# A hybrid diffusion backbone in one core: where the eight PSUM banks are divided and joined, and where the modulation stands

## The chip, the cores and the metric

The kernel runs on one core of one Trainium2 chip. The number that counts is the device time of one execution in microseconds (us). For the kernel before it is 2413.35 us, the median of three runs that lie between 2412.6 and 2416.89 us. Below, the execution that was profiled took 2414.47 us; its span, from the first to the last recorded instruction, is 2412.7 us, so 1.8 us of it lie outside the span.

## The reference, cut to what matters

One inference step of a backbone of two layers. 640 tokens (128 of a prompt and 512 of a sample) with 1024 features pass three sub-layers in each layer: a SwiGLU half step, a mixer (attention beside a gated linear scan in layer 0, a chunked gMLP in layer 1) and a second SwiGLU half step. Each sub-layer normalises before and after and is modulated by a condition:

```python
def rmsnorm(x, g):
    xf = x.astype(jnp.float32)
    y = xf * lax.rsqrt(jnp.mean(xf * xf, axis=-1, keepdims=True) + EPS)
    return (y * g.astype(jnp.float32)).astype(x.dtype)

def adaln(cond, w, b):
    return (jax.nn.silu(cond) @ w + b).reshape(-1, N_SUB, 3, D_MODEL)

def sub_in(x, mod, i, g_pre):
    return rmsnorm(x, g_pre) * (1 + mod[:, i, 1][:, None]) + mod[:, i, 0][:, None]

def sub_out(x, y, mod, i, g_post, coef):
    return x + coef * mod[:, i, 2][:, None] * rmsnorm(y, g_post)

def macaron_ffn(x, mod, i, g_pre, g_post, wg, wu, wd):
    h = sub_in(x, mod, i, g_pre)
    y = (jax.nn.silu(h @ wg) * (h @ wu)) @ wd
    return sub_out(x, y, mod, i, g_post, FFN_RESIDUAL)
```

`adaln` gives 9 x 1024 numbers per layer for each of two conditions, in 72 rows of 128 a layer (called f below). Each f needs its own 512 KB of weights.

## The kernel before, in words

Features lie on the 128 partitions, in eight tiles (`KD`); the 640 tokens are cut into half 0 (384) and half 1 (256). Every weight is float32. ACT writes its rounded high part (L100) and DVE the rest (L101) into a buffer `whl` of which there are six, and a product takes three matmuls: high by high (`hh`), high by low (`hl`), low by high.

The order of instructions on each engine is fixed when the program is built. Every engine takes its queue in that order and waits at the first instruction that isn't ready. Nothing overtakes.

A feed-forward sub-layer (`ffn`) runs over groups of channels. The first group begins in `head`: four blocks of weights for half 0 in four banks at once (the joint product, `gemm_joint`), further blocks one by one, then the same for half 1. DVE takes each bank out (`normed`, L595, the first step of an eviction) and builds `g`. The first down phase follows, whose sums ACT copies to `y` for half 0 and DVE for half 1 (L816, L818). Later groups are "fast": they take products in a few passes from operands made by `fast_operands`, and use two sorts of banks. The last down phase is called by `tail`, first all of half 0, then half 1. While half 1 runs, `chain(0)` works on half 0: the statistics (`rstd`: a matmul with `ones`, L384, and two ACT operations, L393 and L394), then for each of eight feature tiles a scaling (L423), an addition to the residual (L459) and the next operands `hh` on ACT (L430) and `hl` on DVE (L435). What is left of it, and `chain(1)` for half 1, run in the `head` of the next sub-layer, between the evictions. A mixer ends in `out_proj`, which goes through `tail` too.

The eight banks of PSUM are one ring of `ps` tiles or, divided, four `ps` and four `sd`. `split_psum` closes the one ring, opens the two and issues four matmuls with one row into the `sd` banks; `whole_psum` closes both and opens the ring of eight. A bank can be written once the last reader of what it held is through. The division stands in `ffn` behind the first down phase, the join behind `tail`, ahead of the next head. So a head finds eight banks, the four of the joint product and four more.

The modulation goes beside all this: `mod_queue` gives for each f a transfer (L318, on SP's queue, two buffers `wmod`) and two DVE operations (`mod_op`, L326, output `junk`), one for each condition. `pace` spreads them over a feed-forward's units; `out_proj` puts its own behind the units of half 0. `mod_derive` (L367 to L372) makes the factors from the sums.

## Time and profile before

| | |
|---|---|
| median of three runs | 2413.35 us (2412.6 to 2416.89) |
| the profiled execution | 2414.47 us, span 2412.7 us |
| PE (TensorE) busy | 2331.8 us, 97% of the span |
| DVE (VectorE) busy | 1852.1 us, 77% |
| ACT (ScalarE) busy | 1290.0 us, 53% |
| POOL (GpSimd) busy | 327.5 us, 14% |
| mean granted TensorE clock | 0.988 |

In a view of an engine's timeline a row gives the start, the busy time, the line and operation, the tiles and the count; in brackets stand the idle time ahead of it and what ended that idle time. Several instructions of one kind in a row are put into one. The waits of an engine are grouped by what waited and what ended the wait. A row of windows gives for one stretch the busy time of each engine, with counts, and the granted TensorE clock (1.00 is the upper of its two levels, 0.50 the lower).

### The profile page before, as it was taken

The numbers are of one execution on the slowest core, as the hardware profiler recorded it, in microseconds if no ns is written. First come the engines' busy times: TensorE is split into PE (matmuls) and PEld (weight loads), VectorE is DVE, ScalarE is ACT, GpSimd is POOL, SyncE is SP. The second block draws the span as 40 slices with busy tenths as digits, with TensorE's granted clock in tenths as the row PEclk, the third lists the DMA queues.
The fourth block names the chain that finished last, engine by engine and source line by source line (L and its number), as shares of the span: only waits on it lengthen the run. The fifth ranks groups of instructions, "written<-read, shape, count | busy, mean of one in ns | idle before, by whom it ended". The sixth has DMA issues, their size and how long they took to land.

```text
span 2412.7 us, 40104 instructions
## 1 busy us (share of the span) xinstructions
PE 2331.8 (97%) x15528; PEld 2268.6 (94%) x15528; DVE 1852.1 (77%) x3347; ACT 1290.0 (53%) x2637; POOL 327.5 (14%) x289
## 2 busy tenths in 40 slices
PE   7899999999999999999999999999999999999998
PEld 5799999999899799999999999999988899999998
DVE  8898889586966698887875788889495797765574
ACT  4555454565546556544556555445574356454555
POOL 5100000041502340000003100000130540000002
PEclk9999999999999999999999999999999999999999
DMA  8334544431021343353533333443334343332332
GB/s 300 100 120 136 179 136 153 140 126 59 19 77 45 121 143 117 120 174 110 180 123 132 119 109 126 163 151 121 123 123 148 111 135 111 108 114 68 100 97 105
DMA packets 87569, 297.85 MB, mean 123 GB/s; under 512 B 9681, under 2 KB 15313, under 8 KB 84305
## 3 DMA queue, kind: packets, MB, share of 16 engines
q1 hardware_dynamic: 86082, 292.07, 37.0%
q8 instruction: 121, 1.98, 0.3%
q10 hardware_dynamic: 864, 2.17, 0.2%
q0 software_dynamic: 432, 1.05, 0.2%
q14 instruction: 70, 0.57, 0.1%
HBM read 276.25 MB, written 19.01 MB: 122 GB/s over the span
## 4 chain that ended last, share of the span: by engine, by line
PE 65%; DVE 21%; DMA 6%; ACT 4%; issue 3%; POOL 1%; SPq 0%; DVEq 0%; ACTq 0%; POOLq 0%
PE ps L199 35%; PE sd L199 30%; DVE junk L326 4%; DVE whl L101 3%; DMA wmod<-in_wmod 2%; DVE y L423 2%; DVE hl L435 1%; ACT whl L100 1%; DVE hl L631 1%; DMA wraw<-in_wgu 1%; DMA wraw<-in_wd 1%; DMA b<-xspill 1%; DVE b L625 1%; DVE x L459 1%; DMA wraw<-in_wdl 1%
## 5 line engine op out<-in xcount | busy, mean ns | idle before, releaser
L199 PE MATMUL ps<-hh,whl 128*128 128x320 f32 (+4 forms) x4128 | 955.1, 316 | 18.2 <-ACT y L816 8.7
L101 DVE TENSOR_TENSOR whl<-wraw,whl 128x1024 fp32r<-128x1024 f32 (+3 forms) x552 | 531.4, 967 | 328.9 <-ACT whl L100 319.1
L199 PEld LDWEIGHTS ps<-hh,whl 128*128 128x128 f32 x4128 | 710.5, 191 | 25.5 <-ACT y L816 9.3
L199 PE MATMUL ps<-hl,whl 128*128 128x320 f32 (+4 forms) x2064 | 645.1, 313 | 14.5 <-DVE hl L435 13.1
L100 ACT CAST whl<-wraw 128x1024 fp32r<-128x1024 f32 (+3 forms) x552 | 461.5, 839 | 330.1 <-issue 107.4
L199 PE MATMUL sd<-g,whl 128*128 128x384 f32 (+1 forms) x3264 | 482.5, 308 | 5.9 <-DVE g L676 5.3
L199 PEld LDWEIGHTS sd<-g,whl 128*128 128x128 f32 x3264 | 476.9, 188 | 10.4 <-DVE g L676 7.9
L199 PEld LDWEIGHTS ps<-hl,whl 128*128 128x128 f32 x2064 | 395.7, 192 | 19.9 <-DVE hl L435 15.0
L407 POOL TENSOR_TENSOR acc<-acc,tmc 128x384 f32<-128x384 f32 (+1 forms) x154 | 174.4, 1134 | 1766.3 <-ACT tmc L400 1751.2
L199 PE MATMUL sd<-th,whl 128*128 128x320 f32 x2448 | 383.0, 309 | 4.9 <-ACT sd L679 4.9
L199 PEld LDWEIGHTS sd<-th,whl 128*128 128x128 f32 x2448 | 366.2, 188 | 5.7 <-ACT sd L679 5.7
L326 DVE SCALAR_TENSOR_TENSOR junk<-wmod,cbc 128x1024 bf16<-128x1024 f32 x258 | 323.2, 1253 | 30.3 <-DMA wmod<-in_wmod 19.3
L816 ACT COPY y<-sd 128x384 f32<-128x384 f32 (+1 forms) x192 | 80.6, 425 | 113.0 <-PE sd L199 112.9
L199 PE MATMUL ps<-g,whl 128*128 128x384 f32 (+1 forms) x960 | 140.7, 308 | 0.0
L199 PEld LDWEIGHTS ps<-g,whl 128*128 128x128 f32 x960 | 140.1, 188 | 0.3 <-DVE g L743 0.3
L199 PE MATMUL sd<-hh,whl 128*128 128x320 f32 x544 | 131.0, 311 | 0.8 <-DVE tmp L687 0.8
L423 DVE SCALAR_TENSOR_TENSOR y<-y,dm,rstd 128x128 f32<-128x128 f32 (+1 forms) x128 | 70.2, 580 | 34.7 <-ACT rstd L394 34.7
L430 ACT ACTIVATE hh<-x,dm 128x128 fp32r<-128x128 f32 (+1 forms) x144 | 63.5, 468 | 61.1 <-DVE x L459 42.1
L199 PEld LDWEIGHTS sd<-hh,whl 128*128 128x128 f32 x544 | 93.0, 187 | 1.7 <-DVE tmp L687 1.6
L435 DVE SCALAR_TENSOR_TENSOR hl<-x,dm,hh 128x128 fp32r<-128x128 f32 (+1 forms) x144 | 90.1, 656 | 0.7 <-ACT hh L430 0.4
L199 PE MATMUL ps<-whl,hh 128*128 128x320 f32 (+1 forms) x320 | 87.0, 355 | 1.4 <-ACT whl L100 1.4
L786 ACT COPY sd<-y 128x384 f32<-128x384 f32 (+1 forms) x192 | 81.1, 433 | 13.5 <-DVE tmp L690 10.4
(246 smaller groups left out, 2594.2 us busy)
## 6 DMA issues: line engine op xcount, KB each, us to landing
wraw<-in_wgu SPq DMA_DIRECT2D x170, 512.0 KB, 3.8
wmod<-in_wmod SPq DMA_DIRECT2D x130, 512.0 KB, 4.2
wraw<-in_wd SPq DMA_DIRECT2D x64, 320.0 KB, 3.0
xspill<-x SPq DMA_DIRECT2D x12, 1280.0 KB, 4.4
x<-xspill SPq DMA_DIRECT2D x12, 1280.0 KB, 9.2
wraw<-in_wd SPq DMA_DIRECT2D x32, 384.0 KB, 3.8
wraw<-in_wdl SPq DMA_DIRECT2D x24, 512.0 KB, 4.0
b<-xspill SPq DMA_DIRECT2D x16, 640.0 KB, 4.6
```

Source lines behind the costliest of these rows:

```text
L100: k.nc.scalar.copy(w[:, 0, c], raw)
L101: k.nc.vector.tensor_sub(w[:, 1, c], raw, w[:, 0, c])
L199: self.nc.tensor.matmul(out, lhsT, rhs, start=start, stop=stop, **more)
L326: ins = nc.vector.scalar_tensor_tensor(junk, w, 1.0, self.c_bc[:, cond, :], op0=ALU.mult, op1=ALU.mult, accum_out=out)
L407: self.nc.gpsimd.tensor_add(acc, acc, t)
L423: self.nc.vector.scalar_tensor_tensor(self.y[:, m, a:a + ln], src[:, m, a:a + ln], self.mcol(lay, s, which, m, cond), r[:, a - o:a - o + l ...
L430: self.nc.scalar.activation(self.hh[:, k, 2 + a:2 + a + ln], self.x[:, k, a:a + ln], AF.Copy, scale=self.mcol(lay, s, 1, k, cond))
L435: self.nc.vector.scalar_tensor_tensor(self.hl[:, k, 2 + a:2 + a + ln], self.x[:, k, a:a + ln], self.mcol(lay, s, 1, k, cond), self.hh[:, k ...
L459: nc.vector.tensor_add(xs, xs, self.y[:, m, o:o + n])
L625: nc.vector.scalar_tensor_tensor(v, v, self.mcol(lay, s, 1, k + 4 * j, cond), self.r[:, a:a + n], op0=ALU.mult, op1=ALU.mult)
L786: nc.scalar.copy(seeds[m, half][:, :n], self.y[:, m, o:o + n])
L816: nc.scalar.copy(ys, ps[:, :n])
```

## The change

It has three parts. First, `split_psum` stands ahead of the first down phase and no longer behind it, and all sums of that phase are copied by ACT, half 1 too (32 copies move from DVE). Second, `whole_psum` moves out of `ffn` into `head`, ahead of half 1's joint product, if the banks are divided at that point. So half 0 of the three heads that follow a feed-forward sub-layer (of both mixers and of the first half step of layer 1) has four `ps` banks, and the statistics that fall into it take an `sd` bank (`late=True`). The two heads that follow `out_proj` are as they were. Third, `tail` takes a list of modulation steps and puts them behind the units of half 0, with the shifts' operands after them, and the f are dealt out anew:

| place | f before | f after |
|---|---|---|
| ffn(0,0): body, tail | 40, 0 | 32, 5 |
| out_proj(0) | 8 | 11 |
| ffn(0,1): body, tail | 32, 0 | 28, 4 |
| ffn(1,0): body, tail | 32, 0 | 24, 5 |
| out_proj(1) | 8 | 11 |
| ffn(1,1) | 8 | 8 |

```diff
--- before.py
+++ after.py
@@ -376,11 +376,12 @@
         return self.dm[:, j:j + 1]
 
 
-    def rstd(self, half, table, more=None):
+    def rstd(self, half, table, more=None, late=False):
+
 
         nc = self.nc
         n = HALF[half][1]
-        ps = self.ps()
+        ps = self.sd() if late and self.n_sd else self.ps()
         mm = self.nc.tensor.matmul(ps[:, :n], self.ones, self.accs[half], start=True, stop=more is None)
         if more is not None:
             self.mm(ps[:, :n], self.ones, more, False, True)
@@ -448,7 +449,7 @@
 
         nc = self.nc
         o, n = HALF[half]
-        self.rstd(half, 0)
+        self.rstd(half, 0, late=half == 1)
         yield
 
         def f_t(m):
@@ -473,7 +474,7 @@
         if nxt is None:
             return
         yield from self.pipeline(KD, [(0, f_s)])
-        self.rstd(half, 2 if half and nxt != (0, 1) else 0)
+        self.rstd(half, 2 if half and nxt != (0, 1) else 0, late=True)
         yield
 
     def renorm(self, half, nxt):
@@ -523,20 +524,23 @@
                 return
 
 
-    def tail(self, unit, n_blocks, cur, nxt):
+    def tail(self, unit, n_blocks, cur, nxt, mod=()):
 
 
         ws = self.ws
         wis = [ws.next() for _ in range(n_blocks)]
         self.pin(self.nc.scalar.preload_act_table_set(LNEXP))
         ch = [self.chain(0, cur, nxt), self.chain(1, cur, nxt)]
-        if nxt is not None:
-            self.shifts(*nxt)
         both = max(0, n_blocks - NB)
+        mod = list(mod)
         for m in range(KD):
             unit(m, 0, wis)
             if m < both:
                 unit(m, 1, wis)
+            for _ in range(-(-len(mod) // (KD - m))):
+                mod.pop(0)()
+        if nxt is not None:
+            self.shifts(*nxt)
         done = 0
         for m in range(both, KD):
             unit(m, 1, wis)
@@ -578,6 +582,8 @@
                 self.step(ch[1], 99)
             self.step(again[0], 1)
 
+        if self.n_sd:
+            self.whole_psum()
         pss = self.gemm_joint(wis[:joint], self.hacts(1), late)
         self.step(ch[1], 99)
         self.step(again[0], 99)
@@ -694,7 +700,7 @@
         result(tr, sr, r)
 
 
-    def ffn(self, lay, f, ch, mod, nxt, start=None):
+    def ffn(self, lay, f, ch, mod, nxt, start=None, late=()):
         nc, ws = self.nc, self.ws
         s = 0 if f == 0 else 2
         mod = list(mod)[::-1]
@@ -812,13 +818,12 @@
                 end = nxt is None and half == 1
                 if last and not end:
                     self.sq_acc(half, ps[:, :n], m == 0)
-                if gi or half == 0:
-                    nc.scalar.copy(ys, ps[:, :n])
-                else:
-                    nc.vector.tensor_copy(ys, ps[:, :n])
+                nc.scalar.copy(ys, ps[:, :n])
                 if last and end:
                     self.last_part(m, lay, s)
 
+            if gi == 0:
+                self.split_psum()
             if not last:
                 for m in range(KD):
                     wi = ws.next()
@@ -830,14 +835,10 @@
                         self.fast_operands(lay, s, m)
                     else:
                         pace(1)
-                if gi == 0:
-                    self.split_psum()
             else:
                 while mod:
                     mod.pop()()
-                ch = self.tail(down, 6, (lay, s), nxt)
-                self.whole_psum()
-                return ch
+                return self.tail(down, 6, (lay, s), nxt, late)
 
     def open_ffn(self):
         self.g_f, self.fp = self.pool("ffn", side="left")
@@ -1342,11 +1343,9 @@
             ys = self.y[:, m, o:o + n]
             self.sq_acc(half, ps[:, :n], m == 0)
             nc.scalar.copy(ys, ps[:, :n])
-            if half == 0:
-                for _ in range(-(-len(mod) // (KD - m))):
-                    mod.pop(0)()
-
-        return self.tail(unit, KD, (lay, 1), (lay, 2))
+
+        mod.pop(0)()
+        return self.tail(unit, KD, (lay, 1), (lay, 2), mod)
 
 
     def mixer1(self, ch):
@@ -1628,20 +1627,20 @@
             self.mod_load(0)
             self.mod_load(1)
 
-        q = queue(0, (16, 40), (48, 64)) + derive(0, 0, (2,)) + derive(0, 1, (0, 1)) + derive(0, 2, (0, 1))
-        ch = self.ffn(0, 0, None, q, (0, 1), start)
+        q = queue(0, (16, 53))
+        ch = self.ffn(0, 0, None, q[:-10] + derive(0, 0, (2,)) + derive(0, 1, (0, 1, 2)), (0, 1), start, q[-10:])
         self.mixer0(ch)
         self.open_xy()
         self.unspill()
         open_ffn()
-        ch = self.out_proj(0, queue(0, (40, 48)) + derive(0, 1, (2,)))
-        q = queue(0, (64, 72)) + derive(0, 2, (2,)) + queue(1, (0, 24)) + derive(1, 0, (0, 1, 2))
-        ch = self.ffn(0, 1, ch, q, (1, 0))
-        q = queue(1, (24, 40), (48, 64)) + derive(1, 1, (0, 1)) + derive(1, 2, (0, 1))
-        ch = self.ffn(1, 0, ch, q, (1, 1))
+        ch = self.out_proj(0, queue(0, (53, 64)) + derive(0, 2, (0, 1)))
+        q, q1 = queue(0, (64, 72)), queue(1, (0, 24))
+        ch = self.ffn(0, 1, ch, q + derive(0, 2, (2,)) + q1[:-8] + derive(1, 0, (0, 1)), (1, 0), None, q1[-8:] + derive(1, 0, (2,)))
+        q = queue(1, (24, 53))
+        ch = self.ffn(1, 0, ch, q[:-10] + derive(1, 1, (0, 1, 2)), (1, 1), None, q[-10:])
         self.mixer1(ch)
         open_ffn()
-        ch = self.out_proj(1, queue(1, (40, 48)) + derive(1, 1, (2,)))
+        ch = self.out_proj(1, queue(1, (53, 64)) + derive(1, 2, (0, 1)))
         q = queue(1, (64, 72)) + derive(1, 2, (2,))
         ch = self.ffn(1, 1, ch, q, None)
         self.step(ch[0], 99)
```

On DVE in `out_proj(0)` the modulation stands in a row, ahead of the factor for the gate (`dm`), of the first weight block of the next head (`whl_8869`) and of half 0's chain (the `y` and `x` rows). The last rows of it before:

```order
L326 SCALAR_TENSOR_TENSOR junk_8798,modraw<-wmod_8758,cbc_8454 128x1024
L326 SCALAR_TENSOR_TENSOR junk_8834,modraw<-wmod_8758,cbc_8454 128x1024
L367 TENSOR_TENSOR dm<-modraw,cols 128x16
L372 SCALAR_TENSOR_TENSOR dm<-dm,cols 128x16
L101 TENSOR_TENSOR whl_8869<-wraw_8867,whl_8869 128x1024
L423 SCALAR_TENSOR_TENSOR y_8443<-y_8443,dm,rstd 128x384 x2
L459 TENSOR_TENSOR x_8447<-x_8447,y_8443 128x384
L423 SCALAR_TENSOR_TENSOR y_8443<-y_8443,dm,rstd 128x384
```

And in the changed kernel, at the same place:

```order
L326 SCALAR_TENSOR_TENSOR junk_8793,modraw<-wmod_8749,cbc_8435 128x1024
L326 SCALAR_TENSOR_TENSOR junk_8795,modraw<-wmod_8755,cbc_8435 128x1024
L326 SCALAR_TENSOR_TENSOR junk_8831,modraw<-wmod_8755,cbc_8435 128x1024
L367 TENSOR_TENSOR dm<-modraw,cols 128x16
L101 TENSOR_TENSOR whl_8869<-wraw_8867,whl_8869 128x1024
L369 SCALAR_TENSOR_TENSOR dm<-dm,cols 128x16
L424 SCALAR_TENSOR_TENSOR y_8424<-y_8424,dm,rstd 128x384 x2
L460 TENSOR_TENSOR x_8428<-x_8428,y_8424 128x384
L424 SCALAR_TENSOR_TENSOR y_8424<-y_8424,dm,rstd 128x384
```

In the whole stretch from the last blocks of the current product to the first `y` row there are 16 `junk` rows before and 22 after. The first of them stands in both directly behind the last block but one of the current product, so the six more push back everything from `dm` on.

On PE in the middle of the joint products of mixer 1's head (half 0 has 386 columns, half 1 256; `acc` and `ones` are the statistics), with the engines each row waits for in brackets, before:

```order
L199 MATMUL ps_18605<-hh,whl_18506 128x386
L199 MATMUL ps_18605<-hl,whl_18506 128x386
L199 MATMUL ps_18605<-hh,whl_18506 128x386
L384 MATMUL ps_18728<-acc_75,ones 128x384 [waits Pool_49]
L199 MATMUL ps_18804<-hh,whl_18383 128x256 [waits Activation_49]
L199 MATMUL ps_18804<-hl,whl_18383 128x256 [waits DVE_49]
L199 MATMUL ps_18804<-hh,whl_18383 128x256
```

After:

```order
L199 MATMUL ps_18582<-hh,whl_18487 128x386
L199 MATMUL ps_18582<-hl,whl_18487 128x386
L199 MATMUL ps_18582<-hh,whl_18487 128x386
L385 MATMUL sd_18705<-acc_75,ones 128x384 [waits Pool_49]
L199 MATMUL ps_18785<-hh,whl_18364 128x256 [waits DVE_49,Activation_49]
L199 MATMUL ps_18785<-hl,whl_18364 128x256
L199 MATMUL ps_18785<-hh,whl_18364 128x256
```

The statistics went from a `ps` to an `sd` bank, and half 1's first product, which waited for ACT's operands alone, now waits for DVE as well: by the semaphore's count that is the eviction of the fourth bank of half 0.

On PE at the beginning of the first down phase of ffn(0,0) (`g` are its operands, `sd` with `hh` the four one-row matmuls), after:

```order
L199 MATMUL ps_1011<-hl,whl_978 128x256
L199 MATMUL ps_1011<-hh,whl_978 128x256
L199 MATMUL sd_1046<-hh 128x512 [waits DVE_49]
L199 MATMUL sd_1048<-hh 128x512
L199 MATMUL sd_1050<-hh 128x512
L199 MATMUL sd_1052<-hh 128x512
L199 MATMUL ps_1054<-g_103,whl_1058 128x384 [waits Activation_49]
L199 MATMUL ps_1054<-g_103,whl_1058 128x384 x2
```

At the end of the same phase before:

```order
L199 MATMUL ps_1445<-g_106,whl_1426 128x256 x3
L199 MATMUL ps_1445<-g_107,whl_1426 128x256 x3
L199 MATMUL sd_1472<-hh 128x512 [waits DVE_49,Activation_49]
L199 MATMUL sd_1474<-hh 128x512
L199 MATMUL sd_1476<-hh 128x512
L199 MATMUL sd_1478<-hh 128x512
L199 MATMUL ps_1504<-hh,whl_1490 128x320
L199 MATMUL ps_1504<-hl,whl_1490 128x320
```

The four one-row matmuls moved from the end of the phase to its beginning, behind the eviction (on DVE) of the last unit ahead of it.

## Rows read from the trace of the kernel before

**Rows 1.** Page, busy time, share of the span and instructions of the engines.

```profile
PE 2331.8 (97%) x15528; PEld 2268.6 (94%) x15528; DVE 1852.1 (77%) x3347; ACT 1290.0 (53%) x2637; POOL 327.5 (14%) x289
```

**Rows 2.** Waits of PE: us in total, times, longest us.

```profile
PE ps L199 <- ACT y L816: 8.7, 3, 3.5
PE sd L199 <- DVE g L676: 5.3, 8, 0.9
PE sd L199 <- DVE y L818: 5.2, 4, 2.2
PE sd L199 <- ACT sd L679: 4.9, 3, 4.4
```

**Rows 3.** Windows at the lower clock: length, busy times, clock, DMA share, GB/s.

```profile
69.10:79.30 10.20, 4.07 (x17) 3.78 (x18) 9.81 (x29) 4.73 (x18) 4.58 (x5) 0.50 0.10 42
284.20:291.00 6.80, 4.45 (x17) 4.45 (x18) 4.88 (x9) 2.31 (x6) 0.00 (x0) 0.50 0.25 77
```

**Rows 4.** Timeline of PE and DVE where ffn(0,0)'s first down phase begins.

```profile
123.42 0.28 PE L199 MATMUL ps<-hh,whl 128*128 128x256 f32 x1
...
124.70 0.43 DVE L595 TENSOR_TENSOR tmp<-ps,rstd 128x256 f32<-128x256 f32 x1
```

**Rows 5.** Timeline of DVE and PE in the head of mixer 0.

```profile
535.58 0.54 DVE L595 TENSOR_TENSOR tmp<-ps,rstd 128x384 f32<-128x384 f32 x1
...
529.13 0.29 PE L199 MATMUL ps<-hl,whl 128*128 128x256 f32 x1
...
558.82 0.86 PE L199 MATMUL ps<-whl,hh 128*128 128x320 f32 x4 [1.37 <-ACT whl L100]
```

**Rows 6.** Timeline of DVE and PE in the head of ffn(1,0).

```profile
1329.00 1.75 DVE L423 SCALAR_TENSOR_TENSOR y<-y,dm,rstd 128x128 f32<-128x128 f32 x4 [1.14 <-ACT rstd L394]
...
1348.66 0.55 DVE L595 TENSOR_TENSOR tmp<-ps,rstd 128x384 f32<-128x384 f32 x1
...
1343.46 0.29 PE L199 MATMUL ps<-hl,whl 128*128 128x256 f32 x1
```

**Rows 7.** Timeline of DVE and PE in the head of mixer 1.

```profile
1781.78 1.14 DVE L423 SCALAR_TENSOR_TENSOR y<-y,dm,rstd 128x128 f32<-128x128 f32 x4 [3.58 <-ACT rstd L394]
...
1795.46 0.55 DVE L595 TENSOR_TENSOR tmp<-ps,rstd 128x384 f32<-128x384 f32 x1
...
1787.34 0.57 PE L199 MATMUL ps<-hh,whl 128*128 128x256 f32 x1
...
1799.18 0.70 PE L384 MATMUL ps<-acc,ones 128*128 128x256 f32 x2 [1.56 <-POOL acc L407]
```

**Rows 8.** Timeline of DVE and PE, out_proj(0) into the next head.

```profile
838.07 1.91 DVE L326 SCALAR_TENSOR_TENSOR junk<-wmod,cbc 128x1024 bf16<-128x1024 f32 x1
...
843.12 1.22 DVE L326 SCALAR_TENSOR_TENSOR junk<-wmod,cbc 128x1024 bf16<-128x1024 f32 x1
...
847.98 1.23 DVE L326 SCALAR_TENSOR_TENSOR junk<-wmod,cbc 128x1024 bf16<-128x1024 f32 x1 [0.38 <-DMA wmod<-in_wmod]
...
854.91 1.23 DVE L326 SCALAR_TENSOR_TENSOR junk<-wmod,cbc 128x1024 bf16<-128x1024 f32 x1 [1.21 <-DMA wmod<-in_wmod]
...
862.27 1.15 DVE L423 SCALAR_TENSOR_TENSOR y<-y,dm,rstd 128x384 f32<-128x384 f32 x2
...
871.63 1.21 DVE L101 TENSOR_TENSOR whl<-wraw,whl 128x1024 fp32r<-128x1024 f32 x1
...
872.89 0.63 PE L199 MATMUL ps<-hh,whl 128*128 128x386 f32 x2 [0.71 <-DVE whl L101]
```

**Rows 9.** Timeline of DVE and PE, out_proj(1) into the next head.

```profile
1958.56 1.21 DVE L101 TENSOR_TENSOR whl<-wraw,whl 128x1024 fp32r<-128x1024 f32 x1
...
1960.98 0.34 PE L199 MATMUL ps<-hl,whl 128*128 128x386 f32 x1
```

**Rows 10.** Timeline of POOL in out_proj(0).

```profile
831.64 7.25 POOL L407 TENSOR_TENSOR acc<-acc,tmc 128x384 f32<-128x384 f32 x4 [20.84 <-ACT tmc L400]
```

## The prediction

> **What bounds the kernel now.** I read the page first: PE is busy for 97% of the span [rows 1], so what is to be won is small (80.9 us of the span are not PE) and what can be lost is not. The next view was what PE waits for [rows 2]: the three joins cost 8.7 us, the four divisions 5.2, operands of the fast units 4.9 and 5.3. Then I took windows behind long waits, for the granted clock: behind one of 4.4 us the clock is 0.50 for 6.8 us, and PE is busy for 4.45 of them, half of which, 2.2 us, the upper level would have saved [rows 3]. Last, the timelines at the places that the change touches, with the order of both programs beside them: the order says behind what an instruction stands, the trace how late that was. There DVE, 77% busy as a mean, goes on for tens of us with hardly a pause. The chains and the evictions of a head are in such a stretch, so that means say nothing of them.
>
> **The division.** The four waits of 5.2 us at the end of the first down phases go [rows 2]. In their place PE waits at the beginning, until the last unit's bank has been taken out. At ffn(0,0) that unit's last matmul ends at 123.42 + 0.28 = 123.70 and its eviction at 124.70 + 0.43 = 125.13 [rows 4]: 1.4 us, 5.7 at four places. The four one-row matmuls are there before and after. Queued behind the new wait is the whole down phase; nobody but PE waits for it. Net 5.7 - 5.2 = +0.5 us. Ends: -5.2 if nothing new waits; +9.3 if each new wait also brings the 2.2 us of lower clock (0.5 + 4 x 2.2). I take 0.5, since these waits are as long as the old ones. The 32 copies that go to ACT I cost at nothing: ACT is 53% busy, and a copy that comes late is covered by three other banks. Without that cover each would hold up PE by as much as it is late; the upper end has room for that.
>
> **The join.** 8.7 us of waits go [rows 2]. But half 0 of the head now has four banks, all with the joint product, and half 1 can begin only when they are free. So I compare PE's first matmul of half 1 with the end of the last eviction of half 0, which stands in DVE's queue between steps of the second chain.
> - Mixer 0: half 1 began at 529.1 (the second matmul at 529.13); the last eviction ends at 535.58 + 0.54 = 536.1 [rows 5]. DVE has no pause to give up, so 7.0 us later. A later wait of 1.37 us for a weight block [rows 5] is then covered: +5.6.
> - ffn(1,0): 1343.3 (the second matmul at 1343.46) against 1348.66 + 0.55 = 1349.2, 5.9 us. DVE had waited 1.14 us for the statistics [rows 6], and they come earlier without the old join: +4.8. Two units of half 0 also wait for a bank, inside the same time.
> - Mixer 1: 1787.3 against 1796.0, 8.7 us. DVE waited 3.58 us for the statistics, which the join held up: 5.1. A later wait of 1.56 us for POOL is covered [rows 7]: +3.5.
>
> Together +13.9 us, with the 8.7 already inside since I compare times. I let the clock cancel (old joins and new waits are followed alike by a lower clock). Ends: -8.7 if the evictions come early enough for all; +28.2 if nothing is covered and each new wait costs 2.2 at the lower clock (7.0 + 5.9 + 8.7 + 6.6). I take 13.9: DVE's rows follow one another without a pause where the evictions stand.
>
> **The modulation beside out_proj.** Each `out_proj` gets three f more: three transfers on SP's queue and six DVE operations. In DVE's queue they stand ahead of the gate's factor, the first weight blocks of the next head and half 0's chain, so all of that comes later by their time. At least that is 6 x 1.22 = 7.3 us. But the operations wait for their transfers: from 847.98 to 854.91 two f take 6.93 us [rows 8], 3.47 each, 10.4 for three. I take 9.0, about the middle. Is there slack? At out_proj(0) none: the fourth block's low part ends at 871.63 + 1.21 = 872.84, and PE had been waiting 0.71 us for it [rows 8]. So +9.0. At out_proj(1) it ends at 1959.8, while the next head's product begins at 1960.8, its second matmul at 1960.98 [rows 9], and wants the fourth block after nine matmuls of 0.18: 2.6 us of slack, +6.4. Both waits are long enough for a lower clock behind them, 2.2 each as above. Together +19.8 us. Ends: 16.4 (7.3 + 4.7 + 4.4) and 28.4 (10.4 + 7.8 + twice 5.1, half of the 10.2 us at the lower clock that the longest stretch had [rows 3]). SP's queue: the weight transfers behind the `wmod` ones wait in both programs for the splits, so they shift along.
>
> An operation here took 1.91 us at 838.07 while POOL was adding squares, 1.22 at 843.12 [rows 8, 10]. The Trainium skill says, in "GPSIMD Engine Reference", Specifications, that POOL shares its ports to SBUF with DVE and contends with DVE instructions that have two SBUF inputs, as these have. The trace agrees for these two. POOL's work is the same after the change, so by that rule the six more run at the quick rate, and the sum would be 3.4 us lower. The transfers' pace speaks against it.
>
> **The modulation out of the bodies.** 20 f leave three bodies; 14 of them go beside half 0 of a last down phase, where I cost them at nothing: the chain that follows in DVE's queue waits for the statistics, which come from PE at the end of that half. Without that cover a `tail` would lose 1.22 us [rows 8] for each operation, at most ten. What is won is waits of the fast units, where DVE stood before a transfer of an f: the longest is 4.4 us of the 4.9 for `sd` [rows 2], and the 2.2 of lower clock behind it [rows 3]. I take -6.6. Ends: 0 (it turns up elsewhere, since 24 to 32 f stay) and -12.4 (4.9 + 5.3 + 2.2).
>
> On that clock: "TensorE: Matmul & The Clock Gate" in the Trainium skill, Terms, puts the loss at the throttled time times one half at this level, 3.4 us for the 6.8. The rows give less, because PE idled for 2.35 us of that stretch. By the rule this term would be -7.8 and that of out_proj 2.4 higher.
>
> **Sum.** 0.5 + 13.9 + 19.8 - 6.6 = +27.6 us. From the profiled 2414.47 that is 2442.1; the median stands 1.1 below that run, so 2441.0 us.
>
> **Rivals.**
> - A, faster: DVE is not late. With 40 operations gone from the bodies and the old joins gone, it comes to each head early, and the evictions end before PE needs the banks. Price: -5.2 - 8.7 - 12.4 with out_proj at its lower end, +16.4: -9.9, about 2403 us. For it speaks that DVE waited for statistics in two heads [rows 6, 7]. Against it: mixer 1's evictions would have to come up by 8.7 us, its pause gives 3.58. It decides from where mixer 1's fourth eviction ends before half 0's last matmul.
> - B, little slower: the extra f of out_proj hide, because their operations run in DVE's time before the statistics of half 0 are ready. Then 0.5 + 13.9 - 6.6 = +7.8, 2421 us. For it: DVE idles ahead of the first of them. Against it: they stand behind the split of a weight block that comes late from ACT, and the 0.71 us on PE show that the row had no slack [rows 8].
> - C, slower than forecast: nothing is covered, and each wait has its stretch at the lower clock. 0.5 + 28.2 + 28.4 - 6.6 = +50.5, 2464 us. For it: the waits of 7 to 10 us are longer than the one of 4.4. Against it: behind a head PE has waits that a shift covers [rows 5, 7].
> - D, that the division and join do nothing: the order shows new waits on DVE at both places, so this is within the ends above and has no chance of its own.
>
> **Chances and range.** The forecast (2428 to 2456 us) 0.66, A 0.13, B 0.11, C 0.10. Less than 0.2% (4.8 us) can't be told from no change here. Faster by more: A, 0.12. Within it: what A and B have near 2413, 0.05. Slower by more: the forecast, C and the rest of B, 0.83. The range from 2411 to 2458 takes in B and most of the ends, and leaves out A and the far part of C.
>
> **What would show it.** In the profile after: PE waits of about 1.4 us for L601 (the new number of L595) at the four one-row matmuls; in three heads one or two waits of 4 to 8 us at half 1's first matmul, ended by DVE; at the two heads behind out_proj a wait of 6 to 10 us for DVE's split of the fourth block, with 22 `junk` rows ahead of the chain; no wait of 4 us for `sd` near 282 us. It would be wrong if the evictions ended earlier than their place in DVE's queue says, or if out_proj's chain began at 862 as before.

## The result, and the profile after

The changed kernel takes 2435.59 us, the median of six runs (2433.9 to 2441.93), against 2413.65 us for the kernel before in the same job. The ratio is 1.0091, with a 95% interval from 1.0075 to 1.0106: 22 us slower, where 27.6 were forecast. The profiled execution took 2433.9 us with a span of 2432.1; the mean granted clock fell from 0.988 to 0.982.

The page's busy times, which answer to [rows 1]:

```profile
PE 2338.8 (96%) x15528; PEld 2274.7 (94%) x15528; DVE 1852.6 (76%) x3315; ACT 1298.8 (53%) x2669; POOL 328.7 (14%) x289
```

No engine does noticeably more: PE runs as many matmuls as before, and its 7.0 us more of busy time, for the same matmuls, goes with the lower mean clock. So the loss has to be looked for in waits and in the clock. What PE waits for after (total us, times, longest us), to be laid beside [rows 2]:

```profile
PE ps L199 <- DVE tmp L601: 27.1, 5, 11.2
...
PE ps L199 <- DVE whl L101: 4.2, 4, 1.6
...
PE sd L199 <- DVE tmp L601: 3.9, 4, 1.1
...
PE sd L199 <- DVE g L682: 1.3, 2, 0.8
PE sd L199 <- ACT sd L685: 1.0, 1, 1.0
```

What the change was forecast to remove has gone: the waits for `y`, both sorts, and most of the fast units' waits for `g` and `sd`. In their place stands one row of 27.1 us in five waits for L601, the evictions. It is three times the 8.7 us of the old joins. The four waits for L601 in an `sd` bank are the new divisions.

PE's timeline at the first division and at the three joins (start, busy time, what runs, in brackets the idle time ahead and what ended it):

```profile
125.11 0.73 PE L199 MATMUL sd<-hh 1*128 1x512 f32 x2 [0.92 <-DVE tmp L601]
...
519.07 0.66 PE L199 MATMUL ps<-hh,whl 128*128 128x386 f32 x1 [7.20 <-DVE tmp L601]
...
526.66 0.35 PE L199 MATMUL ps<-hh,whl 128*128 128x256 f32 x1 [1.00 <-DVE tmp L601]
...
1344.25 0.66 PE L199 MATMUL ps<-hh,whl 128*128 128x386 f32 x1 [6.88 <-DVE tmp L601]
...
1356.28 0.36 PE L199 MATMUL ps<-hh,whl 128*128 128x256 f32 x1 [0.81 <-DVE tmp L601]
...
1799.35 0.55 PE L199 MATMUL ps<-hh,whl 128*128 128x256 f32 x1 [11.23 <-DVE tmp L601]
```

A matmul of 386 columns belongs to half 0, one of 256 to half 1. So in two heads PE stops already at the fifth block of half 0, for want of a fifth bank, and in mixer 1's head, which has only the joint product, at half 1. The forecast had looked for waits of 4 to 8 us at half 1's first matmul: 7.20 and 6.88 us came earlier, and mixer 1's is 11.23.

To see where the time went, the trace of either kernel was cut at the same instructions, the matmuls of the statistics (L384 before, L385 after), and the lengths compared:

| stages (us in the trace of before) | change in length, us | forecast |
|---|---|---|
| the three joins' surroundings: 487 to 855, 1299 to 1349, 1749 to 1946 | +5.9, +7.8, +5.4 | +5.6, +4.8, +3.5 |
| the two out_proj: 855 to 888, 1946 to 1978 | +9.9, +7.8 | +11.2, +8.6 |
| the three bodies with their divisions: 92 to 487, 888 to 1299, 1349 to 1749 | -9.3, -1.8, -7.5 | -6.1 together |
| all else | +1.2 | 0 |

The second row comes out near the forecast, and the first is 19.1 us where 13.9 were forecast. The third is three times as large as forecast; the experiments on it below say how much of that is real.

### The profile page after: what moved, and what is told of

The parts are those of the page before. It is cut to its first block, busy times and chain, and to the rows that moved or that the text cites. A ratio compares the mean times of both kernels' runs of the same rounds, so it can differ in the third digit from the quotient of the medians.

```text
span 2432.1 us, 40087 instructions
## 1 busy us (share of the span) xinstructions
PE 2338.8 (96%) x15528; PEld 2274.7 (94%) x15528; DVE 1852.6 (76%) x3315; ACT 1298.8 (53%) x2669; POOL 328.7 (14%) x289
## 3 DMA queue, kind: packets, MB, share of 16 engines
q8 instruction: 121, 1.98, 0.3%
## 4 chain that ended last, share of the span: by engine, by line
PE 75%; DVE 15%; DMA 5%; ACT 3%; issue 2%; POOL 0%; SPq 0%; ACTq 0%; DVEq 0%; POOLq 0%
PE ps L199 38%; PE sd L199 36%; DVE junk L326 2%; DVE hl L436 2%; DVE whl L101 2%; DMA wmod<-in_wmod 2%; DVE y L424 2%; DVE x L460 1%; DMA cbc<-in_cc 1%; DMA b<-xspill 1%; ACT whl L100 1%; DMA wraw<-in_wgu 1%; DVE kx L1046 0%; DVE cv L1414 0%; DVE hl L637 0%
## 5 line engine op out<-in xcount | busy, mean ns | idle before, releaser
L199 PE MATMUL ps<-hh,whl 128*128 128x320 f32 (+4 forms) x4128 | 959.7, 316 | 43.3 <-DVE tmp L601 27.1
L199 PE MATMUL ps<-hl,whl 128*128 128x320 f32 (+4 forms) x2064 | 648.2, 314 | 16.4 <-DVE hl L436 15.0
L424 DVE SCALAR_TENSOR_TENSOR y<-y,dm,rstd 128x128 f32<-128x128 f32 (+1 forms) x128 | 70.9, 584 | 28.2 <-ACT rstd L395 28.2
```

The lines of the kernel that those rows point to most:

```text
L199: self.nc.tensor.matmul(out, lhsT, rhs, start=start, stop=stop, **more)
L424: self.nc.vector.scalar_tensor_tensor(self.y[:, m, a:a + ln], src[:, m, a:a + ln], self.mcol(lay, s, which, m, cond), r[:, a - o:a - o + l ...
```

## The experiments

The kernel before differs a little from job to job (medians of 2413.65, 2413.26, 2411.3 and 2410.29 us), so kernels of different jobs are compared by their ratios to it. 0.001 is 2.4 us.

**Each part alone.** Three kernels, each the kernel before with one part of the diff. The division alone:

```diff
+            if gi == 0:
+                self.split_psum()
             if not last:
...
-                if gi == 0:
-                    self.split_psum()
```

(with all copies on ACT, as in the change).

> The kernel before with the first part of the change alone: division ahead of the first down phase, half 1's sums copied by ACT; join and modulation as before. Theory (read from both traces: four waits of 3.9 us in place of 5.2, and 3.4 us less at the lower clock, half of it lost): 3 us faster, 2408 to 2413. Rival (a ring of four banks with all copies on ACT holds PE up in that phase, and the gain in the changed kernel's bodies came from the modulation): no faster than before, 2413 or more.

Measured: 2413.65 us, ratio 1.0002 (0.9988 to 1.0016). No effect that can be told: the theory's 3 us did not come, and the 32 copies on ACT show no price. PE's waits at the four divisions became

```profile
PE sd L199 <- DVE tmp L596: 3.7, 4, 1.0
```

instead of 5.2 us [rows 2]: one sort of wait for another of nearly the same length.

The join alone:

```diff
+        if self.n_sd:
+            self.whole_psum()
         pss = self.gemm_joint(wis[:joint], self.hacts(1), late)
...
-                ch = self.tail(down, 6, (lay, s), nxt)
-                self.whole_psum()
-                return ch
+                return self.tail(down, 6, (lay, s), nxt, late)
```

> The kernel before with the second part alone: join ahead of half 1 in the next head; division and modulation as before. Theory (evictions late in DVE's queue, and a long stretch at the lower clock behind each wait): 15 to 22 us slower, about 2432, with three waits of 6 to 11 us ended by DVE's L601. Rival (it is the modulation operations in the tails that made DVE late for these heads): less than 10 us slower, under 2424.

Measured: 2427.35 us, ratio 1.006 (1.0038 to 1.0083), +14.5 us, at the lower edge of the theory's range. The waits for the evictions are there with the join alone:

```profile
PE ps L199 <- DVE tmp L598: 26.1, 4, 11.5
```

So they don't come from the modulation, which here lies as before.

The modulation alone (the new lists of f, and `tail` with its list):

```diff
+        mod = list(mod)
         for m in range(KD):
...
+            for _ in range(-(-len(mod) // (KD - m))):
+                mod.pop(0)()
```

> The kernel before with the third part alone: f dealt out anew, 5, 4 and 5 of them beside half 0 of last down phases, 11 in each out_proj; banks as before. Theory (from the two traces: about 15 us won in the bodies, about 18 lost behind the two out_proj): -2 to +6 us, 2411 to 2420. Rival (the sizes of the forecast, 6.6 won and 19.8 lost, the rest of the bodies' gain being the division's): 10 to 16 us slower, 2424 to 2430.

Measured: 2417.99 us, ratio 1.0027 (1.0013 to 1.0040), +6.5 us: the theory's time, half a microsecond above its difference, and below the rival's. The three parts add up: 0.5 + 14.5 + 6.5 = 21.5 of the 22 measured together. Each is uncertain by 3 to 5 us, so that they might still overlap by a few.

**What the modulation is made of.** First the changed kernel with the six f taken out of out_proj and put back in the bodies:

```diff
-        q = queue(0, (16, 53))
+        q = queue(0, (16, 56))
...
-        ch = self.out_proj(0, queue(0, (53, 64)) + derive(0, 2, (0, 1)))
+        ch = self.out_proj(0, queue(0, (56, 64)) + derive(0, 2, (0, 1)))
```

and the same in layer 1.

> The changed kernel with 8 f in each out_proj as before, the other 6 in the bodies of ffn(0,0) and ffn(1,0) (35 and 27). Theory (the parts add up; division and modulation with 8 f gave -10.7 us, the join alone +14): 2414 to 2421, 15 to 21 us under the changed kernel. Rival (division and join and the modulation in out_proj lean on one another: DVE is late in the heads anyway, so less comes back): 2425 or more.

Measured: 2421.97 us, ratio 1.0044 (1.0029 to 1.0059), 11 us less than the changed kernel, between the two expectations. That is the price of the six f in out_proj, less what they cost in the bodies: by the stages of the two traces 14.6 us less behind the two out_proj and 3.6 more in the bodies. The stage of out_proj(0) still takes 36.6 us there and 36.3 with the join alone, against 33.5 to 34.4 in the kernels with the old join and 8 f; so the join has a price there too, and the parts overlap a little.

Then three kernels on the modulation alone. In the first, 20 f leave the bodies and are computed nowhere, and out_proj keeps its 8:

```diff
-        q = queue(0, (16, 53))
+        q = queue(0, (16, 48))
...
-        q, q1 = queue(0, (64, 72)), queue(1, (0, 24))
+        q, q1 = queue(0, (64, 72)), queue(1, (0, 20))
...
-        q = queue(1, (24, 53))
+        q = queue(1, (24, 48))
```

> Division, join and everything else as before; of the modulation only the bodies change: 20 f (8 in the first body, 4 in the second, 8 in the third) are left out, with their transfers and their DVE operations, and computed nowhere (their factors are zero). Theory: the bodies themselves win about 18 us, as the stages of the changed kernel showed, since DVE stood there before transfers in the middle of its queue. Then 2394 to 2397 us. Rival, the forecast's term of -6.6 us: 2405 to 2409 us; the rest of the 18 would then be an effect of other stages.

Measured: 2401.85 us, ratio 0.996 (0.9947 to 0.9974), -9.7 us, between the two expectations. In the second, the 14 f of the tails are back:

```diff
-        ch = self.out_proj(0, queue(0, (53, 64)) + derive(0, 2, (0, 1)))
+        ch = self.out_proj(0, queue(0, (56, 64)) + derive(0, 2, (0, 1)))
```

(likewise in layer 1; these six f alone are left out).

> As the run of the bodies alone, but 14 of the 20 f are computed in the last down phases, as in the changed kernel; the 6 f of out_proj are left out. Theory: the tails' operations are covered, so the time is that of the run of the bodies alone, within 3 us, 2394 to 2400 us; and the modulation alone (2418 us) stands about 17 us or more above it, which is the price of three f more in each out_proj. Rival: a tail pays for its operations, 28 times 1.22 us at the most, so up to 34 us above the run of the bodies alone, above 2404 us.

Measured: 2398.76 us, ratio 0.9952 (0.9939 to 0.9965), -11.6 us, as the theory had it. The tails' 28 operations cost nothing that can be seen; the rival's 34 us for them is excluded. And the modulation alone lies 0.0075 above this kernel: three more f in each out_proj cost 18.1 us, with an uncertainty of about 4.4. By the stages of the two traces it is 16.3.

The windows of the three bodies summed up (length, then the busy times), before:

```profile
sum 1204.17, PE 1188.01 PEld 1180.11 DVE 956.72 ACT 634.78 POOL 27.07; mean PE 396.00 PEld 393.37 DVE 318.91 ACT 211.59 POOL 9.02
```

in the changed kernel:

```profile
sum 1185.60, PE 1181.06 PEld 1176.81 DVE 937.93 ACT 639.64 POOL 29.40; mean PE 393.69 PEld 392.27 DVE 312.64 ACT 213.21 POOL 9.80
```

with the tails but without the six f:

```profile
sum 1189.28, PE 1182.43 PEld 1178.45 DVE 949.21 ACT 634.05 POOL 28.77; mean PE 394.14 PEld 392.82 DVE 316.40 ACT 211.35 POOL 9.59
```

The bodies are 18.6 and 14.9 us shorter in these executions. PE's idle time in them (length less busy) falls from 16.2 us to 4.5 and 6.9, and its busy time by 5.6 to 7.0, since fewer stretches are at the lower clock. But the times say -9.7 and -11.6 for the whole kernel. The reason is in the other traces. The division alone and the join alone have the same f in their bodies as before, and yet in their profiled executions the bodies are shorter by 7.5 and 11 us:

```profile
sum 1196.63, PE 1183.42 PEld 1175.10 DVE 949.08 ACT 640.97 POOL 27.06; mean PE 394.47 PEld 391.70 DVE 316.36 ACT 213.66 POOL 9.02
sum 1193.12, PE 1182.88 PEld 1176.64 DVE 953.39 ACT 633.65 POOL 27.08; mean PE 394.29 PEld 392.21 DVE 317.80 ACT 211.22 POOL 9.03
```

and the modulation alone:

```profile
sum 1184.67, PE 1180.91 PEld 1176.68 DVE 946.96 ACT 633.69 POOL 28.91; mean PE 393.64 PEld 392.23 DVE 315.65 ACT 211.23 POOL 9.63
```

So with the same f the bodies of three executions differ by 11 us, and those of the kernel before are the longest. The mean of the three with the old lists is 1198.0 us, of the three with the new ones (the changed kernel, the modulation alone, the kernel without the six f) 1186.5: 11.5 us, as the runs say. Of these, 8.2 are idle time of PE and 3.3 its busy time. This part is worth 10 to 12 us, by the intervals of the runs 6 to 15.

The third asks what in out_proj has the price, transfers or operations. The last three f of each out_proj read the buffer of the eighth, so their factors are wrong:

```diff
-                hold[i] = self.mod_dma(lay, fs[i])
+                hold[i] = self.mod_dma(lay, fs[i]) if i < n else hold[n - 1]
```

> The modulation of the changed kernel alone, but the last three f of each out_proj have no transfers of their own: their DVE operations read the buffer of the eighth f (so these factors are wrong). Theory: the price of an f more in out_proj is set by the pace of transfers, 3.6 us each against 2.44 us of operations, so each out_proj is 3 to 4 us shorter than with the modulation alone, 2409 to 2413 us. Rival: the operations alone set it, or the transfers collide with those of the weights only; then no difference at out_proj, 2416 to 2419 us.

Measured: 2413.03 us, ratio 1.0006 (0.9995 to 1.0017), 5 us below the modulation alone, with an uncertainty of 4. DVE, the last `junk` row and the first row of half 0's chain; with transfers:

```profile
859.52 1.22 DVE L326 SCALAR_TENSOR_TENSOR junk<-wmod,cbc 128x1024 bf16<-128x1024 f32 x1
...
862.10 1.14 DVE L424 SCALAR_TENSOR_TENSOR y<-y,dm,rstd 128x384 f32<-128x384 f32 x2
```

without:

```profile
857.60 1.23 DVE L326 SCALAR_TENSOR_TENSOR junk<-wmod,cbc 128x1024 bf16<-128x1024 f32 x1
...
860.33 1.14 DVE L424 SCALAR_TENSOR_TENSOR y<-y,dm,rstd 128x384 f32<-128x384 f32 x2
```

Counted from the statistics' matmul ahead of it (846.14 and 845.66 us), the chain begins 1.3 us earlier without transfers. It stands 8.7 and 7.4 us behind its place before, and 7.4 is six operations of 1.23. So six sevenths of the delay are DVE's own work and one the transfers' pace. The stage itself, up to the next statistics, is only 0.5 us shorter at out_proj(0) and 0.6 longer at out_proj(1): the time lies at the theory's edge, the stages with the rival. Whether the 5 us of the times come from here stays open.

**What the join waits for.** Two kernels change when the evictions of half 0 stand in DVE's queue. In the first they begin three steps of the second chain earlier:

```diff
-EV = 3
+EV = 0
```

> The changed kernel with the evictions of half 0 from the first step of the second chain on (EV = 0 for 3), so that in the order of DVE the fourth stands some 4 us of work earlier in mixer 1's head. Theory (PE waits for the evictions' place in DVE's queue): the waits for L601 in the heads fall from 27.1 to 12 to 21 us and the time by 4 to 12 us, 2424 to 2432. Rival (the statistics of half 0, which come from ACT late, hold the evictions wherever they stand): the waits stay above 24 us, the time at 2433 or more.

Measured: 2439.91 us, ratio 1.012 (1.0105 to 1.0136), 7 us above the changed kernel by ratio, 4 by median. The theory fell. PE's waits:

```profile
PE ps L199 <- DVE tmp L601: 24.8, 5, 9.1
...
PE ps L385 <- POOL acc L408: 4.6, 3, 3.7
```

The evictions won 2.3 us, nearly all in mixer 1's head, where PE then waited 3.7 us for POOL's sums of half 1, which the second chain on DVE feeds. The heads behind out_proj changed as well: out_proj(0)'s stage is 1.8 us longer, with a wait of 3.95 us for `hh` where the changed kernel has 2.38. In the second kernel they are written ahead of all steps of that chain:

```diff
-            if i >= EV and (i - EV) % 2 == 0 and todo:
...
+        for i in range(joint):
             evac(i, 0, pss[i])
+        self.step(ch[1], 10)
```

> The changed kernel, but in every head the four evictions of half 0 stand ahead of all steps of the second chain, in a row, and no longer between them. Theory: the waits at the joins are the evictions' place in DVE's queue; they end 4 to 8 us earlier in three heads and the time falls to 2418 to 2428 us. Rival, as when they were moved by three steps: what the evictions win the second chain loses, PE waits for operands of half 1 instead (hl, whole waits for L601 and hl together above 30 us as in the changed kernel's 42), 2432 to 2442 us. The two heads behind out_proj change too, where the evictions have banks to spare: there it can only lose.

Measured: 2437.36 us, ratio 1.011 (1.0095 to 1.0125), not faster than the changed kernel; the rival's time. PE's waits:

```profile
PE ps L199 <- DVE tmp L596: 25.1, 5, 9.1
...
PE ps L385 <- POOL acc L408: 4.8, 2, 3.8
```

DVE in mixer 1's head of this kernel:

```profile
1790.80 1.07 DVE L436 SCALAR_TENSOR_TENSOR hl<-x,dm,hh 128x128 fp32r<-128x128 f32 x2
1791.79 1.47 DVE L596 TENSOR_TENSOR tmp<-ps,rstd 128x384 f32<-128x384 f32 x3
...
1794.57 0.55 DVE L596 TENSOR_TENSOR tmp<-ps,rstd 128x384 f32<-128x384 f32 x1
```

and in the changed kernel:

```profile
1794.03 1.01 DVE L601 TENSOR_TENSOR tmp<-ps,rstd 128x384 f32<-128x384 f32 x2
...
1796.75 0.54 DVE L601 TENSOR_TENSOR tmp<-ps,rstd 128x384 f32<-128x384 f32 x1
...
1798.66 0.54 DVE L601 TENSOR_TENSOR tmp<-ps,rstd 128x384 f32<-128x384 f32 x1
```

The evictions now stand nearly together, but steps of the second chain still run ahead of the first of them, so that this is no full test of the order. (An eviction needs half 0's statistics; that this is why the steps stand ahead is not shown.) The statistics' matmul there begins 2.05 us earlier than in the changed kernel (1785.25 against 1787.30), so of the 4.09 us between the last evictions 2.0 are a real gain. After that PE waits 3.8 us for POOL's sums of half 1, which come from the chain that was pushed back; the rival had looked for waits for `hl`, and none stands in the three heads. Mixer 1 (1749 to 1946 us in the trace of before) is 5 us longer than in the changed kernel, with either order. So moving the evictions exchanged one wait for another. That the amount of DVE's work in the head is the bound is argued from this, not shown: a kernel that takes work off DVE there was not tried.

**What the clock costs behind a join.** Matmuls whose results nobody uses fill PE's wait, 30 in the heads of mixer 0 and ffn(1,0), 46 in that of mixer 1:

```diff
+        if self.n_sd:
+            t, w = self.sd(), self.ws.get(wis[0])
+            for _ in range(46 if n_a == joint else 30):
+                self.mm(t, w[:, 0, 0:P], w[:, 0, 0:512])
         for i in range(joint, n_a):
```

> The changed kernel with matmuls whose result nobody uses (30 of 512 columns in the heads of mixer 0 and ffn(1,0), 46 in mixer 1's) in an sd bank, where PE waits in the three heads; they take no longer than the waits of 7.2, 6.9 and 11.2 us. Theory (the lower clock behind each wait costs by itself: PE was busy 4.4, 5.5 and 4.4 us in those stretches, half of it lost): the three stretches go and the time falls by 5 to 8 us, to 2428 to 2431. Rival (behind the wait PE runs after DVE anyway, and the lower clock costs nothing): 2434 or more, stretches gone or not.

Measured: 2436.28 us, ratio 1.0107 (1.0092 to 1.0122): no gain in the whole kernel, against the theory. Windows around the second and third join of the changed kernel (length, busy times of PE, PEld, DVE, ACT and POOL, granted clock, DMA share, GB/s):

```profile
1339.50:1349.70 10.20, 5.45 (x17) 5.48 (x18) 10.20 (x30) 8.54 (x21) 3.71 (x5) 0.50 0.35 145
1793.50:1803.70 10.20, 4.35 (x20) 4.38 (x21) 10.20 (x28) 8.51 (x19) 3.62 (x4) 0.50 0.47 194
```

and with the filling:

```profile
1339.50:1349.70 10.20, 10.11 (x47) 8.30 (x46) 10.20 (x32) 8.09 (x22) 3.12 (x4) 1.00 0.32 131
...
1358.70:1362.10 3.40, 3.40 (x18) 3.40 (x18) 0.56 (x1) 0.50 (x1) 0.00 (x0) 0.50 0.00 0
...
1796.00:1803.00 7.00, 6.18 (x29) 4.81 (x27) 7.00 (x24) 6.70 (x17) 1.73 (x3) 1.00 0.53 222
```

In these two heads the filling did what it should: the clock is 1.00 where it was 0.50, but for 3.4 us at ffn(1,0) behind half 1's own wait. Yet mixer 1's stage is only 1.8 us shorter and ffn(1,0)'s 0.1 longer. Where that comes from is in half 1's first row and the statistics that end the stages, in the changed kernel:

```profile
1362.11 0.59 PE L385 MATMUL ps<-acc,ones 128*128 128x256 f32 x2
...
1807.08 0.59 PE L385 MATMUL ps<-acc,ones 128*128 128x256 f32 x2
```

and with the filling:

```profile
1357.96 0.36 PE L199 MATMUL ps<-hh,whl 128*128 128x256 f32 x1 [1.87 <-DVE tmp L605]
1365.30 0.59 PE L385 MATMUL ps<-acc,ones 128*128 128x256 f32 x2
...
1802.95 0.35 PE L199 MATMUL ps<-hh,whl 128*128 128x256 f32 x1 [0.82 <-DVE tmp L605]
1808.79 0.59 PE L385 MATMUL ps<-acc,ones 128*128 128x256 f32 x2
```

In mixer 1 half 1 begins at the same place of the stage as without filling, since the wait is DVE's, and then takes 5.8 us in place of 7.7 (1799.35 to 1807.08): the lower clock had cost 1.9, near half of the 4.35 us that PE was busy in that stretch. In ffn(1,0) half 1 begins 1.4 us earlier in its stage, behind a longer wait (1.87 us, before 0.81), and with the clock low behind that wait it takes 7.3 us in place of 5.8 (1356.28 to 1362.11). There the lower clock only moved. So the rival's time came, but not its reason: behind a join the lower clock does cost PE, by about half of its busy time in the stretch and not of the stretch's length. In mixer 0 the filling pushed half 1 back (a wait of 6.3 us there), and the head lost 4.7 us; there it was no clean test, and it hides the gain in the kernel's time.

**Versions without the bad parts.** The division, and the modulation with 8 f in each out_proj, with the join where it was:

```diff
-        ch = self.out_proj(0, queue(0, (53, 64)) + derive(0, 2, (0, 1)))
+        ch = self.out_proj(0, queue(0, (56, 64)) + derive(0, 2, (0, 1)))
...
+                ch = self.tail(down, 6, (lay, s), nxt, late)
+                self.whole_psum()
+                return ch
```

> Division ahead of the first down phase and modulation beside half 0 of the last down phases, but only 8 f in each out_proj (35 and 27 in the bodies of ffn(0,0) and ffn(1,0)); join as before. Theory: what the bodies win stays and the loss behind out_proj is gone: 10 to 17 us faster than before, 2397 to 2404. Rival 1 (out_proj loses by the new place of its f in the program, not by their number): 2410 or more. Rival 2 (the bodies win only since 6 f are in out_proj): 3 to 5 us faster.

Measured: 2402.54 us, ratio 0.9958 (0.9945 to 0.9971): the theory's range, and faster than the kernel before by 10 us, than the changed one by 32. Both rivals fell. With 9 f in the tails of the two first half steps and 4 in each out_proj:

```diff
-        ch = self.out_proj(0, queue(0, (56, 64)) + derive(0, 2, (0, 1)))
+        ch = self.out_proj(0, queue(0, (60, 64)) + derive(0, 2, (0, 1)))
```

> Division ahead of the first down phase, join as before, 9 f in place of 5 beside half 0 of the last down phases of ffn(0,0) and ffn(1,0), 4 f in place of 8 in each out_proj, bodies of 35 and 27 f. Theory (a tail's DVE is idle while PE works, up to some 25 operations; behind out_proj 8 f were already at the edge, 0.7 us of wait): 0 to 4 us faster than with 5 and 8 f, 2398 to 2403. Rival (18 operations push the chain of half 0 back in the tails): 2405 to 2415.

Measured: 2401.52 us, ratio 0.9964 (0.9952 to 0.9975). It is in the theory's range and can't be told from the one before it. In its profile out_proj(0)'s stage is 1.9 us shorter than with 8 f and out_proj(1)'s the same, while PE waits 0.5 us for POOL's sums at the end of half 0 in the first tail. So at out_proj(1) four f fewer than 8 won nothing.

## Why the prediction held, step by step

| term | forecast (ends) | measured, by the ratios of the runs |
|---|---|---|
| division | +0.5 (-5.2 to +9.3) | +0.5 (-2.9 to +3.9) |
| join | +13.9 (-8.7 to +28.2) | +14.5 (+9.2 to +20.0) |
| three f more in each out_proj | +19.8 (16.4 to 28.4) | +18.1, uncertain by 4.4 |
| out of the bodies, into the tails | -6.6 (-12.4 to 0) | -11.6 (-14.7 to -8.4) |
| sum, and the changed kernel | +27.6 | +22.0 (+18.1 to +25.6) |

**The division** came out by its mechanism: the new waits [rows 4] are 3.9 us at the four places, 0.9 to 1.1 each where 1.4 were expected. The last unit's matmul ends at 123.91 + 0.28 = 124.19, so the eviction began 0.45 us behind it and not 1.0 us as before:

```profile
123.91 0.28 PE L199 MATMUL ps<-hh,whl 128*128 128x256 f32 x1
...
124.64 0.42 DVE L601 TENSOR_TENSOR tmp<-ps,rstd 128x256 f32<-128x256 f32 x1
```

**The join** was read rightly as a comparison of two times: when PE wants half 1 and when the fourth eviction is through. Measured from the start of their stages, half 1 begins 6.4, 7.8 and 6.5 us later than before (526.66, 1356.28 and 1799.35 us against 529.1, 1343.3 and 1787.3, corrected by the stages' shifts of -8.8, +5.2 and +5.5). Forecast were 7.0, 5.9 and 8.7, and the two later waits that were to be covered, 1.37 and 1.56 us, are gone. PE's idle time in the three stages grew by 4.0, 5.1 and 5.4 us, 14.5 together where 13.9 were forecast (5.6, 4.8 and 3.5: the sum is nearer than its parts). "DVE has no pause to give up" held. Where it had one, in mixer 1 [rows 7], the pause is gone:

```profile
1784.27 1.88 DVE L424 SCALAR_TENSOR_TENSOR y<-y,dm,rstd 128x128 f32<-128x128 f32 x4
```

"I let the clock cancel" is the step that did not hold: behind the new waits the clock is low for 6.8, 10.2 and 10.2 us and behind the old joins for 3.4, 0 and 3.4, and PE's busy time in the three stages is 1.9, 2.7 and 0.0 us longer for the same matmuls. With these 4.6 us the stages come to 19.1. The runs put the join alone at 14.5 (9.2 to 20.0), which can't tell 13.9 from 19.1; that the forecast is so near their middle is luck in part. Rival A needed evictions that come early, and none do. C needed nothing to be covered and 2.2 us of clock behind each wait; two waits were covered, and the clock cost 4.6 in all.

The Trainium skill ("TensorE: Matmul & The Clock Gate", Terms) takes the loss as the throttled time times one half at this level. For the 17.0 us that the filling took away at the second and third join (10.2 + 10.2 - 3.4) that would be 8.5 us; the stages gave back 1.7. The trace disagrees with the rule where PE idles in such a stretch: in the two of 10.2 us it was busy for 5.45 and 4.35.

**out_proj** is where the clock cost most. PE's rows behind out_proj(0), to be laid beside the last of [rows 8]:

```profile
869.69 0.44 PE L199 MATMUL ps<-hh,whl 128*128 128x386 f32 x1 [2.38 <-ACT hh L431]
871.71 0.58 PE L199 MATMUL ps<-hl,whl 128*128 128x386 f32 x1 [1.57 <-DVE hl L436]
...
874.84 0.69 PE L199 MATMUL ps<-hh,whl 128*128 128x386 f32 x1 [0.62 <-DVE whl L101]
875.82 0.69 PE L199 MATMUL ps<-hh,whl 128*128 128x386 f32 x1 [0.29 <-ACT whl L100]
...
877.98 1.01 PE L199 MATMUL ps<-hh,whl 128*128 128x386 f32 x2 [1.15 <-DVE whl L101]
```

and the windows at the lower clock behind the two out_proj:

```profile
871.60:881.80 10.20, 8.03 (x22) 6.61 (x23) 10.20 (x15) 7.35 (x14) 4.36 (x4) 0.51 0.48 154
...
1977.80:1984.60 6.80, 6.03 (x19) 6.03 (x20) 6.80 (x9) 4.45 (x8) 4.18 (x3) 0.50 0.53 159
```

The size was right and its form was not. "A wait of 6 to 10 us for the split of the fourth block" did not appear. The delay is paid in five waits of 6.0 us at out_proj(0), the first two for the chain's operands, where there were 0.7 before, and 3.8 us at out_proj(1). The rest is PE's busy time, 4.6 and 4.0 us more for the same matmuls, and most of that is the clock: PE is busy for 8.03 and 6.03 us of the two stretches, half of which, 4.0 and 3.0, the upper level would have saved. 5.3 + 4.6 and 3.8 + 4.0 are the stages' +9.9 and +7.8. The forecast had 9.0 and 6.4 of waits and 2.2 of clock at each. So it had 6.3 us too much for the waits and about 4 too little for the clock, and that its sum came out near is luck. The first step rested on a chain that begins 9.0 us later; DVE's rows after:

```profile
860.90 1.23 DVE L326 SCALAR_TENSOR_TENSOR junk<-wmod,cbc 128x1024 bf16<-128x1024 f32 x1 [1.08 <-DMA wmod<-in_wmod]
...
867.38 1.14 DVE L424 SCALAR_TENSOR_TENSOR y<-y,dm,rstd 128x384 f32<-128x384 f32 x2
```

From the start of its stage, the chain's first row comes 8.0 us later than at 862.27 before [rows 8], between the 7.3 of the operations alone and the 9.0 that were taken. The extra operations ran at the quick rate, as forecast (the last four rows 1.22 to 1.23 us each). So rival B fell: nothing of the extra f hides.

**The bodies** are the term that was mis-sized: "I take -6.6" counted one stall of 4.4 us and its clock, where -11.6 were won. The stall that was counted is there in all three traces with the old lists, and in none of the three with the new ones. Before, DVE stands ahead of it before a transfer:

```profile
278.39 1.23 DVE L326 SCALAR_TENSOR_TENSOR junk<-wmod,cbc 128x1024 bf16<-128x1024 f32 x1 [3.21 <-DMA wmod<-in_wmod]
```

With the division alone and the join alone that wait is 2.58 and 1.98 us, and the clock is low for 3.4 us behind it, before for 6.8. The term left out the many smaller waits: PE's waits for `g` and `sd` were 10.2 us before [rows 2], 8.2 and 6.3 in those two, and 1.5 to 2.5 with the new lists. The tails' operations cost nothing, as forecast. This step's value lies within its ends. By the runs it is 5.0 of the 5.6 us between 27.6 and 22.0.

## What to carry to other kernels

Where a bank, a buffer or an operand changes hands, compare two times from the trace: when the waiting engine wants it, and when the releasing instruction ends, by its place in its engine's queue; the mean load of that engine says nothing there. Work put ahead of a chain that another engine waits for was paid in waits and in the clock behind them (six operations of 1.2 us cost stages of 9.9 and 7.8 us), and the same work beside a stretch that waits for something else cost nothing that could be seen (28 operations in the tails). Price each part of a mixed change by itself: here one part lost 14.5 us, one did nothing, and of the third one half won 11.6 and the other lost 18.1, so that leaving out the losing parts gave a kernel 10 us faster than the one before. And a sum that comes out near is no proof of its terms: under this one the bodies were 5 us off, and at the joins and behind out_proj the clock was forecast too small.

## What was not expected of the hardware

- Behind the joins, 17.0 us at 0.50, taken away in two heads, shortened their stages by only 1.8 and -0.1 us. The loss went by PE's busy time in the stretch (1.9 us of 4.35 busy in mixer 1's 10.2), and at ffn(1,0) the lower clock came back behind the next wait, of 1.87 us.
- One profiled execution overstated a part: the bodies were 14.9 us shorter in the trace of a kernel that is 11.6 us (8.4 to 14.7) faster as a whole. With the same f, the bodies took 1193.1, 1196.6 and 1204.2 us in three executions.
